# Seven-product groups of a hybrid layer: sums made in three PSUM banks, product order turned

## The chip, the cores and the metric

The kernel runs on one core of one Trainium2 chip. The metric is device time in microseconds (us) of one execution. The engines are called as the profile calls them: PE is the matrix engine, DVE the vector engine, ACT the scalar engine, POOL and SP the two others (here mostly queues that issue transfers). PSUM is the memory into which PE writes its products, in banks of 128 partitions x 512 fp32 numbers.

## The reference, cut to what matters

One layer on 512 tokens of 2048 channels, fp32 in and out. The projection `h @ w_in` has 7 x 1024 columns; half of the layer is a causal depthwise convolution of width 31, the other half attention with 16 heads of 64.

```python
h = rms_norm(x, norm_g)
z = h @ w_in                       # (512, 2048) @ (2048, 7168)
a_val, a_glu, a_gate, q, k, v, b_gate = jnp.split(z, SPLIT_POINTS, axis=-1)
u = causal_depthwise_conv(a_val * sigmoid(a_glu), conv_w, conv_b)
u = silu(layer_norm(u)) @ conv_pw_w + conv_pw_b
y_a = u * silu(a_gate)
q, k = rms_norm per head of q and k
o = dilated_attention_mixture(q, k, v)   # three dilated windows, mixed
y_b = o * silu(b_gate)
y = x + concat(y_a, y_b) @ w_out
```

## The kernel before

**Tiles and groups.** Everything stays on the core: tokens lie in 16 tiles of 128 channels x 512 tokens (`x16`). The columns of `w_in`, of the pointwise matrix and of `w_out` are worked off in groups of 512 columns, named by `GROUPS`: four of the gated value (`vg`, 0 to 3), then `q0`, `k0`, `v0`, a gate, the second halves, the pointwise groups and the output. A group of `w_in` has four units of 512 x 512 weights (1 MB each), which SP fetches into a ring of eight tiles `wf`. Products are made in fp16 with each operand as a high and a low part: `tri` issues three matmuls (high x high, high x low, low x high), L411, L412 and L413. For the high parts ACT copies with a scale (`hi`, L1128), for the low parts DVE subtracts (`lo`; every DVE instruction passes through a helper and has L80).

**Seven products.** Three groups, `vg3`, `q0` and `v0`, cut x and the weights into 2 x 2 blocks and make seven block products in place of eight (Strassen's scheme in Winograd's form), in `input_products`. s1 to s4 are sums of weight blocks, t1 to t4 sums of blocks of x (made early by `sum_x`, on DVE). Each product has two pairs of units and, in each, two halves m of 128 columns or tokens: 4 pieces of 12 matmuls of 256 columns. One piece is one *slot*. So such a group has 28 slots, and slot 4n + 2 pair + m holds piece (pair, m) of product n. Each product has a bank of its own out of the four of `lin_ps`. Results leave the bank by an ACT copy (L1180) or a DVE operation that also adds, and the four output blocks are then put together by DVE.

**What sets the order.** The order is written by hand. The list `plan` in `input_products` gives each step a slot relative to the group's first; `after(n, fn)` enters it into a calendar that is worked off clock by clock, and all engines execute in the order in which the calendar issued their instructions. In one clock the steps of the calendar are issued ahead of the matmuls that come later in `plan`. `hi` of a weight block stands five slots ahead of its product, `lo` four (the second product's first half one later). Three of the four weight sums are made by POOL as adding transfers (`nc.gpsimd.dma_start` with `accum_op`, L1122), s1 by DVE.

**The filler.** The convolution is 30 steps for each of 8 tiles on DVE (`cv<-u,cw,cv`, one multiply-add each), issued by `run_conv` wherever the class `Weighed` thinks that DVE has room: each DVE instruction adds 180 plus its size to a load, each clock takes 1230 (later 1480) off it, and conv steps are issued while it is below zero. The sum of the convolution's tiles (`lnacc`) ends in one matmul for the mean, L568.

**q and k.** `norm_qk` makes the per-head norm: a square (ACT, L1242 in `q0`, L510 in `k0`), a sum (DVE, `ss`), mean and epsilon on POOL (L478), a power on POOL (L168), a scaling (DVE), the high part (ACT, `qhl`, L486), the low part (DVE), then transposing transfers issued by SP, one for each part.

Of the kernel before, what the change touches and what calls it, by code (L numbers as in the profile page):

```python
# [70 lines left out]
class Weighed:  # L71
# [5 lines left out]
    def __getattr__(self, name):  # L77
        def call(out, src, *args, **kw):
            self.load += START + max(math.prod(a.shape[1:]) for a in (out, src) if hasattr(a, "shape"))
            return getattr(self.engine, name)(out, src, *args, **kw)  # L80
        return call
# [3 lines left out]
def layer(ctx: ExitStack, tc: tile.TileContext, xt, w1, w2, w3, g_in, conv_w, conv_b,  # L85
# [273 lines left out]
    xn, tx = {}, {}  # L359

    def sum_x(j):
# [9 lines left out]
        V.tensor_sub(t4, b21, t2)
        both = lambda t: t.rearrange("p (n t) -> p n t", n=2)

        def high():
            for n, t in ((0, t12), (2, t34)):
                A.activation(to[:, n:n + 2, 0], both(t), AF.Copy)

        def low():
# [30 lines left out]
    def tri(ps, a, b, first, last):  # L409
        (ah, al), (bh, bl) = a, b  # L410
        T.matmul(ps, ah, bh, start=first, stop=False)  # L411
        T.matmul(ps, ah, bl, start=False, stop=False)  # L412
        T.matmul(ps, al, bh, start=False, stop=last)  # L413
# [53 lines left out]

    by_head = lambda t: t.rearrange("p (h d) -> p h d", d=DH)

    def norm_qk(store, z, sq, n, to):  # L470
# [13 lines left out]
        def high():  # L484
            got["hl"] = temp("qhl", F16, [P, 2, S])
            A.activation(got["hl"][:, 0], z, AF.Copy)  # L486

        def low():
            hl_t = got["hl"]
            V.tensor_tensor(hl_t[:, 1], z, hl_t[:, 0], op=OP.subtract)  # L490
            for part in range(2):
                if store not in qk:
                    qk[store] = [wide_tile("qk4", [P, 4, S], F16) for _ in range(2)]
                to(qk[store][part], hl_t[:, part])
# [610 lines left out]

    def input_products(i0):
# [9 lines left out]
        def add(name, pair):
            if name == "s1":
                V.tensor_tensor(block("a11", pair), block("a22", pair), block("a11", pair), op=OP.subtract)
            else:
                x, to = SUMS[name]  # L1120
                if name in BY_DMA:
                    nc.gpsimd.dma_start(block(to, pair), block(x, pair), accum_op=OP.add)  # L1122
                else:
# [26 lines left out]
        order = [("p1", "a11", "b11"), ("u", "a22", "t4"), ("x", "a12", "b21"), ("p7", "s3", "t3"), ("p5", "s1", "t1"),  # L1150
                 ("p6", "s2", "t2"), ("z", "s4", "b22")]
        u_first = group != SEVEN[0]
        if u_first:
            order[:2] = order[1::-1]

        def product(n, pair, m):
            to, w, x = order[n]
            if (pair, m) == (0, 0):
                bank[to] = lin_ps.tile([P, 2, H], F32, name="ps_l", tag="ps_l")
            ps, ms = bank[to][:, m], slice(m * P, (m + 1) * P)  # L1160
            for k in range(KU):
                t, xs = weights[w, pair], x_part(x, pair, k)
                first, last_ = pair == m == k == 0, pair == m == 1 and k == KU - 1
                if by_token:
                    tri(ps, [x[:, ms] for x in xs], (t[:, 0, k], t[:, 1, k]), first, last_)
                else:
                    tri(ps, [t[:, j, k, ms] for j in range(2)], xs, first, last_)
# [10 lines left out]
        def copy(name):  # L1178
            t = got[name] = slot("cb")
            A.activation(t, bank.pop(name).rearrange("p m t -> p (m t)"), AF.Copy, scale=e["p"])  # L1180

        def stt(out, name, by, other, op):
            V.scalar_tensor_tensor(out, bank[name].rearrange("p m t -> p (m t)"), e[by], other, op0=OP.mult, op1=op)

        def first_block():
            got["11"] = slot("cb")
            stt(got["11"], "x", "p", got["p1"], OP.add)
            bank.pop("x")

        def joint():  # L1190
            q, h = got["p1"], got["p7"]
            stt(q, "p6", "p", q, OP.subtract)
            bank.pop("p6")
# [261 lines left out]
```

## Time and profile before

| what | before |
| --- | --- |
| median of 3 runs | 817.36 us (817.11 to 817.39) |
| profiled execution, first to last instruction (span) | 815.8 us |
| PE busy | 807.9 us, 99% |
| DVE busy | 707.1 us, 87% |
| ACT busy | 553.6 us, 68% |
| POOL busy | 138.1 us, 17% |
| granted PE clock | 0.999 |

Of the profiled execution the span is what is recorded; the 1.56 us between it and the median lie ahead of the first and behind the last instruction. A line of a timeline reads: start, duration, engine, line, operation, output<-inputs, sizes, and in brackets how long the engine was idle before it and on whom it waited. Successive instructions of one engine overlap a little at their ends, so the distance between two starts is what counts.

### The profile page before, as it was taken

The numbers are of one execution on the slowest core, as the hardware profiler recorded it, in microseconds if no ns is written. First come the engines' busy times: TensorE is split into PE (matmuls) and PEld (weight loads), VectorE is DVE, ScalarE is ACT, GpSimd is POOL, SyncE is SP. The second block draws the span as 40 slices with busy tenths as digits, with TensorE's granted clock in tenths as the row PEclk, the third lists the DMA queues.
The fourth block names the chain that finished last, engine by engine and source line by source line (L and its number), as shares of the span: only waits on it lengthen the run. The fifth ranks groups of instructions, "written<-read, shape, count | busy, mean of one in ns | idle before, by whom it ended". The sixth has DMA issues, their size and how long they took to land.

```text
span 815.8 us, 13495 instructions
## 1 busy us (share of the span) xinstructions
PE 807.9 (99%) x5271; PEld 500.6 (61%) x5271; DVE 707.1 (87%) x1181; ACT 553.6 (68%) x778; POOL 138.1 (17%) x159
## 2 busy tenths in 40 slices
PE   9999999999999999999999999999999999999998
PEld 6887645888646864444444444444444444788887
DVE  6768999889888989999999988996677798998985
ACT  6667687567656678677756748487688858766540
POOL 0001020413223500004112010010110002412420
PEclk9999999999999999999999999999999999999999
DMA  9953343995675862537473632536343477578752
GB/s 341 344 215 102 105 110 98 132 279 113 261 143 114 156 252 98 122 104 174 136 181 100 172 105 86 134 104 168 104 117 104 136 236 234 116 176 189 130 104 66
DMA packets 98625, 125.62 MB, mean 154 GB/s; under 512 B 62720, under 2 KB 83968, under 8 KB 89344
## 3 DMA queue, kind: packets, MB, share of 16 engines
q1 hardware_dynamic: 80800, 107.38, 41.9%
q0 software_dynamic: 17472, 17.30, 14.9%
q8 instruction: 41, 0.67, 0.3%
q14 instruction: 24, 0.20, 0.1%
q10 hardware_dynamic: 288, 0.07, 0.0%
HBM read 88.56 MB, written 4.19 MB: 114 GB/s over the span
## 4 chain that ended last, share of the span: by engine, by line
PE 69%; DVE 19%; ACT 5%; issue 3%; DMA 3%; POOL 1%; SPq 0%; ACTq 0%; DVEq 0%; POOLq 0%
PE ps_l L411 17%; PE ps_l L412 17%; PE ps_l L413 16%; PE ps_l L879 10%; DVE cv L80 6%; DVE wl L80 3%; DVE ws L80 3%; ACT junk L190 2%; PE ps_s L413 2%; PE ps_s L411 2%; PE ps_s L412 2%; PE ps_s L723 2%; PE ps_o L763 2%; DMA wf<-w_dram 1%; DVE cb L80 1%
## 5 line engine op out<-in xcount | busy, mean ns | idle before, releaser
L80 DVE SCALAR_TENSOR_TENSOR cv<-u,cw,cv 128x511 f32<-128x511 f32 (+14 forms) x240 | 162.2, 728 | 0.4 <-ACT cv L544 0.4
L190 ACT ACTIVATE junk<-wf 128x2048 uint8<-128x2048 f32 x68 | 129.2, 1900 | 3.5 <-DMA wf<-w_dram 3.1
L411 PE MATMUL ps_l<-x,wh 128*128 128x512 f16 x320 | 121.4, 379 | 0.3 <-DVE glu L80 0.3
L413 PE MATMUL ps_l<-x,wl 128*128 128x512 f16 x320 | 121.3, 379 | 0.0
L412 PE MATMUL ps_l<-x,wh 128*128 128x512 f16 x320 | 121.3, 379 | 0.0
L299 ACT ACTIVATE wh<-wf,ws 128x2048 f16<-128x2048 f32 x44 | 87.7, 1993 | 49.0 <-PE ps_l L412 49.0
L80 DVE SCALAR_TENSOR_TENSOR wl<-wf,ws,wh 128x2048 f16<-128x2048 f32 x45 | 105.6, 2347 | 13.0 <-ACT wh L299 13.0
L411 PE MATMUL ps_l<-wh,x 128*128 128x512 f16 x256 | 97.1, 379 | 0.0
L412 PE MATMUL ps_l<-wl,x 128*128 128x512 f16 x256 | 97.1, 379 | 0.0
L413 PE MATMUL ps_l<-wh,x 128*128 128x512 f16 x256 | 97.0, 379 | 0.0
L80 DVE SCALAR_TENSOR_TENSOR ws<-wf,ws 128x1024 f16<-128x1024 f32 x70 | 89.0, 1278 | 7.5 <-ACT ws L1128 4.9
L411 PEld LDWEIGHTS <-wh 128*128 128x128 f16 x480 | 47.0, 98 | 55.4 <-issue 3.5
L413 PEld LDWEIGHTS <-wl 128*128 128x128 f16 x480 | 46.9, 98 | 53.6 <-DVE wl L80 0.4
L412 PEld LDWEIGHTS <-wh 128*128 128x128 f16 x480 | 46.9, 98 | 50.4 <-issue 0.7
L879 PE MATMUL ps_l<-xr,wr 128*128 128x512 f32 x288 | 69.7, 397 | 0.1
L204 POOL TENSOR_SCALAR ws<-ws 128x1 f32<-128x1 f32 x22 | 10.7, 485 | 341.8 <-DVE ws L80 313.0
L879 PEld LDWEIGHTS ps_l<-xr,wr 128*128 128x128 f32 x288 | 54.1, 189 | 13.8 <-ACT xr L338 1.0
L413 PEld LDWEIGHTS <-x 128*128 128x128 f16 x352 | 34.4, 98 | 32.8 <-issue 1.5
L411 PEld LDWEIGHTS <-x 128*128 128x128 f16 x352 | 34.4, 98 | 32.4 <-issue 1.9
L412 PEld LDWEIGHTS <-x 128*128 128x128 f16 x352 | 34.4, 98 | 30.6 <-issue 0.5
L946 ACT ACTIVATE ws<-wf,ws 128x1024 f16<-128x1024 f32 x28 | 32.1, 1147 | 28.7 <-PE ps_l L413 9.4
L1128 ACT ACTIVATE ws<-wf,ws 128x1024 f16<-128x1024 f32 x42 | 46.4, 1138 | 6.1 <-PE ps_l L413 3.9
(250 smaller groups left out, 1823.3 us busy)
## 6 DMA issues: line engine op xcount, KB each, us to landing
wf<-w_dram SPq DMA_DIRECT2D x72, 1024.0 KB, 5.2
wf<-wf POOLq DMA_DIRECT2D x30, 512.0 KB, 6.5
x<-xt_dram SPq DMA_DIRECT2D x16, 256.0 KB, 6.7
res<-xt_dram SPq DMA_DIRECT2D x8, 512.0 KB, 6.5
out_dram<-res SPq DMA_DIRECT2D x15, 256.0 KB, 2.2
wf<-w_dram SPq DMA_DIRECT2D x7, 512.0 KB, 7.2
wf<-wf POOLq DMA_DIRECT2D x6, 256.0 KB, 6.3
qk<-qhl SPq DMA_TRANSPOSE x40, 3.0
```

The costliest lines, as they stand in the source:

```text
L80: return getattr(self.engine, name)(out, src, *args, **kw)
L190: A.activation(junk[:, :n], src, AF.Square, scale=scale, accum_out=acc)
L204: G.tensor_scalar(scale, scale, 1e-30, 2.0 ** (-2 * top), op0=OP.max, op1=OP.mult)
L299: A.activation(parts[i][0], raw[i], AF.Copy, scale=wscale[units[i][3:]][0])
L411: T.matmul(ps, ah, bh, start=first, stop=False)
L412: T.matmul(ps, ah, bl, start=False, stop=False)
L413: T.matmul(ps, al, bh, start=False, stop=last)
L723: T.matmul(ps[i, a], qk["q", hf][q][rows, p4, i * P:w], qk["k", hf][k][rows, p4, :w], start=n == 0, stop=n == 2)
L763: T.matmul(po[rows, i * P:(i + 1) * P], vs[hf][j // 2][:, j % 2, 2 * p4 + a, vp * DH:(vp + 1) * DH], got["t", a][:, pp * (ALL // P) + FROM ...
L879: T.matmul(banks[group, m], wt[:, a, m * P:(m + 1) * P], xk[b], start=k == 0 and a == b == 0, stop=k == KC - 1 and a == 1)
L946: A.activation(t[:, 0], block(name), AF.Copy, scale=wscale["wa", g][0])
L1128: A.activation(t[:, 0], block(name, pair), AF.Copy, scale=wscale[group][0])
```

## The change

In the three groups the seven products are made in the order a11 b11, a12 b21, s1 t1, s2 t2, s3 t3, s4 b22, a22 t4, in three banks A, C, B, A, A, B, A. A bank is no longer emptied after each product: products 4, 5 and 7 are added by PE to what stands in A, product 6 to what stands in B. What is needed of the partial sums is copied out between: A after product 1 (`p1`), B after product 3 (`p5`), A after product 4 (`u2`, in two copies of 256 columns at slots 15 and 16, while slots 15 and 16 are the last piece of product 4 and the first of product 5), A after product 5 (`nw`), A at the end. DVE combines three times per group instead of seven. The signs of t2, t3, t4 change with it, so `sum_x` has two multiply-subtract operations where it had an add and a subtract; t1 and t2 now lie in tiles of one pool, t3 and t4 in tiles of another. The weight sums are s1, s2 and s4 by transfers and s3 by DVE; s2 is now at slots 0 and 1. `hi` and `lo` of the second product's first half come one slot earlier. The measuring of newly fetched weights is spread (offsets 0, -1, +2, +3).

For q and k the high and the low part lie side by side in one tile, and one transpose takes both; mean and epsilon go from POOL to DVE. `Weighed` counts 90 for operations under 256 numbers and 25/24 of the size.

```diff
-            self.load += START + max(...)
+            n = max(math.prod(a.shape[1:]) for a in (out, src) if hasattr(a, "shape"))
+            self.load += (START if n >= H else START // 2) + n * 25 // 24
...
-        V.tensor_sub(t3, b12, b22)
-        V.tensor_add(t2, b22, t1)
-        V.tensor_sub(t4, b21, t2)
+        V.tensor_sub(t3, b22, b12)
+        V.scalar_tensor_tensor(t2, t1, -1.0, b22, op0=OP.mult, op1=OP.subtract)
+        V.scalar_tensor_tensor(t4, t2, -1.0, b21, op0=OP.mult, op1=OP.subtract)
...
+    def turn_qk(to, t, src):
+        nc.sync.dma_start(to[:, :, :, t * P:(t + 1) * P].rearrange("p d h t -> p (d h) t"),
+                          src.rearrange("p d h t -> p (d h t)"), transpose=True)
...
-            G.tensor_scalar(ss, ss, f / DH, f * RMS_EPS, op0=OP.mult, op1=OP.add)
+            V.tensor_scalar(ss, ss, f / DH, f * RMS_EPS, op0=OP.mult, op1=OP.add)
...
+    IN_SUMS = {"s1": ("a22", "a21"), "s2": ("a21", "a11"), "s4": ("a11", "a12")}
+    IN_PLACE = {"s1": "a21", "s2": "a11", "s3": "a21", "s4": "a12"}
+    ORDER = (("A", "a11", "b11"), ("C", "a12", "b21"), ("B", "s1", "t1"), ("A", "s2", "t2"), ("A", "s3", "t3"),
+             ("B", "s4", "b22"), ("A", "a22", "t4"))
...
-            if (pair, m) == (0, 0):
+            if to not in bank:
                 bank[to] = lin_ps.tile([P, 2, H], F32, name="ps_l", tag="ps_l")
...
-                    after(MEASURE, lambda j=j: measure(i0 + j + RING))
+                    after(MEASURE + (0, -1, 2, 3)[j], lambda j=j: measure(i0 + j + RING))
...
+        def copy(to, name, by="p", f=0, n=S):
+            if f == 0:
+                got[to] = slot("cb")
+            A.activation(got[to][:, f:f + n], flat(name)[:, f:f + n], AF.Copy, scale=e[by])
+
+        def joint(to, name, other):
+            got[to] = got.pop(other)
+            V.scalar_tensor_tensor(got[to], flat(name), e["p"], got[to], op0=OP.mult, op1=OP.add)
+            bank.pop(name)
+
+        def fourth():
+            p5 = got.pop("p5")
+            got["22"] = got.pop("nw")
+            V.tensor_tensor(got["22"], got["22"], p5, op=OP.subtract)
+
+        def third():
+            copy("21", "A", "n")
+            bank.pop("A")
...
-                norm_qk(group, t, sq, [(2, 4, 5, 6), (2, 5, 6, 8), (3, 8, 9, 11), (2, 9, 10, 12)][n], to)
+                norm_qk(group, t, sq, (2, 5, 6, 8), to)
...
+        plan = [(2, scales_of), (4, lambda: copy("p1", "A")), (8, lambda: joint("11", "C", "p1")), (18 if kind == "v" else 9, lambda: out("11")),
+                (12, lambda: copy("p5", "B")), (15, lambda: copy("u2", "A", n=H)), (16, lambda: copy("u2", "A", f=H, n=H)),
+                (20, lambda: copy("nw", "A", "n")), (21, fourth), (22, lambda: out("22")),
+                (24, lambda: joint("12", "B", "u2")), (25, lambda: out("12")), (28, third), (29, lambda: out("21"))]
...
-                at = 4 * n + 2 * pair - 5 + ((n, pair) == (1, 0))
+                at = 4 * n + 2 * pair - 5
```

How the instructions stand now is shown at three places. On PE in `vg3`, around slot 16 of the group (`tx` are the sums of x, `ws` the weight parts, L411 to L413 before and L413 to L415 now the three matmuls of `tri`; the last rows of one slot and the first of the next). Before:

```order
L411 MATMUL ps_l<-tx,ws 128x256
L412 LDWEIGHTS ws
L412 MATMUL ps_l<-tx,ws 128x256
L413 LDWEIGHTS ws
L413 MATMUL ps_l<-tx,ws 128x256
L411 LDWEIGHTS ws [waits Activation_49]
L411 MATMUL ps_l<-tx,ws 128x256 [waits PE_49]
L412 LDWEIGHTS ws
L412 MATMUL ps_l<-tx,ws 128x256
L413 LDWEIGHTS ws [waits DVE_49]
```

And now:

```order
L413 MATMUL ps_l<-tx,ws 128x256
L414 LDWEIGHTS ws
L414 MATMUL ps_l<-tx,ws 128x256
L415 LDWEIGHTS ws
L415 MATMUL ps_l<-tx,ws 128x256
L413 LDWEIGHTS ws
L413 MATMUL ps_l<-tx,ws 128x256 [waits Activation_49]
L414 LDWEIGHTS ws
L414 MATMUL ps_l<-tx,ws 128x256
L415 LDWEIGHTS ws [waits DVE_49]
```

Before, the slot's first weight load waited for the weight part that ACT makes five slots ahead, and the matmul only for PE's own earlier work. Now the matmul itself waits for ACT, and what it waits for is the copy of the `u2` half that is issued just ahead of it. The same row with the same wait stands 12 matmuls earlier, at the start of slot 15, and both stand again in `q0` and in `v0`: six rows in all.

On ACT in `q0`, around its slots 12 to 17 (L1180 and L1189 empty a bank, L1128 and L1138 are `hi`, L486 and L494 the high part of q; L190 and L191 measure fetched weights). Before:

```order
L1242 ACTIVATE sq<-cb 128x512 [waits DVE_49]
L1128 ACTIVATE ws<-wf,ws 128x1024 [waits PE_49,Activation_49]
L1128 ACTIVATE ws<-wf,ws 128x1024 [waits DMASW0_49,PE_49,Activation_49]
L1180 ACTIVATE cb<-ps_l,esc 128x512 [waits PE_49]
L486 ACTIVATE qhl<-cb 128x512 [waits DVE_49]
L1128 ACTIVATE ws<-wf,ws 128x1024 [waits DMASW1_49,Activation_49]
```

And now:

```order
L1189 ACTIVATE cb<-ps_l,esc 128x512 [waits PE_49]
L1138 ACTIVATE ws<-wf,ws 128x1024 [waits DVE_49,Activation_49]
L494 ACTIVATE qhl<-cb 128x4x128 [waits DVE_49]
L1189 ACTIVATE cb<-ps_l,esc 128x256 [waits PE_49]
L1138 ACTIVATE ws<-wf,ws 128x1024 [waits DMASW2_49,Activation_49]
L1189 ACTIVATE cb<-ps_l,esc 128x256 [waits PE_49]
```

The first of the two `u2` copies stands right behind `qhl`, which waits for DVE; before, `qhl` stood behind the copy.

On DVE at the start of `v0` (`z` and `ss` belong to `k0`, whose last results are then taken out of PSUM; `ws<-wf,ws` are `lo` of the first products of `v0`). Before:

```order
L80 SCALAR_TENSOR_TENSOR z<-ps_l,esc,qg 128x512 [waits PE_49]
L80 SCALAR_TENSOR_TENSOR ws<-wf,ws 128x1024 [waits DMAHW5_49,Activation_49]
L80 SCALAR_TENSOR_TENSOR cv<-u,cw,cv 128x484 [waits DVE_49]
L80 SCALAR_TENSOR_TENSOR z<-ps_l,esc,qg 128x512 [waits PE_49]
L80 SCALAR_TENSOR_TENSOR cv<-u,cw,cv 128x483 [waits DVE_49]
L80 SCALAR_TENSOR_TENSOR ws<-wf,ws 128x1024 [waits DMAHW6_49,Activation_49]
L80 SCALAR_TENSOR_TENSOR ws<-wf,ws 128x1024 [waits DMAHW4_49,Activation_49]
```

And now:

```order
L81 SCALAR_TENSOR_TENSOR z<-ps_l,esc,qg 128x512 [waits PE_49]
L81 SCALAR_TENSOR_TENSOR ws<-wf,ws 128x1024 [waits DMAHW2_49,Activation_49]
L81 SCALAR_TENSOR_TENSOR z<-ps_l,esc,qg 128x512 [waits PE_49]
L81 SCALAR_TENSOR_TENSOR ws<-wf,ws 128x1024 [waits DMAHW1_49,Activation_49]
L81 SCALAR_TENSOR_TENSOR cv<-u,cw,cv 128x482
L81 SCALAR_TENSOR_TENSOR ws<-wf,ws 128x1024 [waits DMAHW3_49,Activation_49]
```

The third `ws` (the first half of the second product) stands a slot earlier, and one conv step in place of two lies between the rows shown.

More of the change, by code (lines that the diff above doesn't have):

```diff
@@ L32 @@
 LP = 4
+H = S // 2
 WARM = 9
@@ L406, in token_rsqrt, with tri @@
         A.activation(row, ps, AF.Copy)
-    def tri(ps, a, b, first, last):
+    def tri(ps, a, b, first, last, more=False):
         (ah, al), (bh, bl) = a, b
-        T.matmul(ps, ah, bh, start=first, stop=False)
-        T.matmul(ps, ah, bl, start=False, stop=False)
-        T.matmul(ps, al, bh, start=False, stop=last)
+        T.matmul(ps, ah, bh, start=first, stop=False, skip_group_check=more)
+        T.matmul(ps, ah, bl, start=False, stop=False, skip_group_check=more)
+        T.matmul(ps, al, bh, start=False, stop=last, skip_group_check=more)
     u, cv, bg, ag = {}, {}, {}, {}
@@ L484, in high @@
         def high():
-            got["hl"] = temp("qhl", F16, [P, 2, S])
-            A.activation(got["hl"][:, 0], z, AF.Copy)
+            got["hl"] = temp("qhl", F16, [P, NT, 2, P])
+            A.activation(got["hl"][:, :, 0], by_block(z), AF.Copy)
         def low():
             hl_t = got["hl"]
[L490 to L494, printed above, removed]
+            V.tensor_tensor(hl_t[:, :, 1], by_block(z), hl_t[:, :, 0], op=OP.subtract)
+            if store not in qk:
+                qk[store] = [wide_tile("qk4", [P, 2, 2, S], F16) for _ in range(2)]
+            to(qk[store], hl_t)
         for m, fn in zip(n, (reduce, scale, high, low)):
@@ L514, in evac_qk @@
         norm_qk(("k" if is_k else "q", half_i), z, sq, n,
-                lambda to, src: nc.sync.dma_start(to[:, :, t * P:(t + 1) * P], src, transpose=True))
+                lambda to, src: [turn_qk(to[x], t, src[:, 2 * x:2 * x + 2]) for x in range(2)])
     vscale = {}
@@ L722, in scores @@
                     for a, rows in enumerate(halves):
-                        T.matmul(ps[i, a], qk["q", hf][q][rows, p4, i * P:w], qk["k", hf][k][rows, p4, :w], start=n == 0, stop=n == 2)
+                        T.matmul(ps[i, a], qk["q", hf][p4 // 2][rows, p4 % 2, q, i * P:w],
+                                 qk["k", hf][p4 // 2][rows, p4 % 2, k, :w], start=n == 0, stop=n == 2)
             for i in order:
@@ L1148, in x_part @@
             return [t[:, f:f + H] for t in x16[8 * pair + 4 * (name[1] == "2") + k]]
[L1150 to L1154, printed above, removed]
         def product(n, pair, m):
[L1157 to L1158 removed]
+            to, w, x = ORDER[n]
+            if to not in bank:
                 bank[to] = lin_ps.tile([P, 2, H], F32, name="ps_l", tag="ps_l")
             ps, ms = bank[to][:, m], slice(m * P, (m + 1) * P)
+            opens = n == [o[0] for o in ORDER].index(to)
             for k in range(KU):
                 t, xs = weights[w, pair], x_part(x, pair, k)
[L1163 removed]
+                first, last_ = opens and pair == m == k == 0, pair == m == 1 and k == KU - 1
                 if by_token:
[L1165 removed]
+                    tri(ps, [x[:, ms] for x in xs], (t[:, 0, k], t[:, 1, k]), first, last_, not opens)
                 else:
[L1167 removed]
+                    tri(ps, [t[:, j, k, ms] for j in range(2)], xs, first, last_, not opens)
         def scales_of():
@@ L1176, in scales_of @@
             e.update(p=p, n=n)
[L1178 to L1193, printed above, removed]
-            V.tensor_tensor(h, h, q, op=OP.add)
-        def fifth():
-            got["22"] = slot("cb")
-            stt(got["22"], "p5", "n", got["p7"], OP.add)
-            stt(got["p1"], "p5", "p", got["p1"], OP.subtract)
-            bank.pop("p5")
-            got["12"] = got.pop("p1")
-        def sixth():
-            t = got["21"] = got.pop("u")
-            V.tensor_tensor(t, t, got.pop("p7"), op=OP.add)
-        def final():
-            stt(got["12"], "z", "p", got["12"], OP.add)
-            bank.pop("z")
+        flat = lambda name: bank[name].rearrange("p m t -> p (m t)")
+        def copy(to, name, by="p", f=0, n=S):
[13 more added lines that the diff above has]
+            bank.pop("A")
         count = [0]
```

51 lines of the change are left out of this document (22 added, 29 removed).

## The prediction, made before the run

> **What bounds the kernel now.** I read the page's first part, then PE's waits, then the three changed groups as windows. The page:
>
> ```profile
> span 815.8 us, 13495 instructions
> PE 807.9 (99%) x5271; PEld 500.6 (61%) x5271; DVE 707.1 (87%) x1181; ACT 553.6 (68%) x778; POOL 138.1 (17%) x159
> ```
>
> PE is busy 99% of the span, and the change leaves it the same matmuls. So an edit gains only where PE now stands still, and loses wherever it makes PE stand still. The list of PE's waits (who waited <- for whom: us, times, longest) says where it does:
>
> ```profile
> PE ps_l L412 <- DVE ws L80: 1.8, 2, 1.1
> PE ps_s L568 <- DVE lnacc L80: 0.8, 1, 0.8
> PE ps_l L411 <- ACT ws L1128: 0.4, 1, 0.4
> PE ps_l L411 <- DVE glu L80: 0.3, 1, 0.3
> ```
>
> These 3.3 us are all that stands in the list after PE's start. Short waits hide behind matmuls whose modelled ends overlap, so I also compare the three groups, which have the same 336 matmuls (window, its length, busy time of PE, PEld, DVE, ACT, POOL, granted clock, DMA share, GB/s):
>
> ```profile
> 138.60:175.30 36.70, 36.70 (x338) 32.86 (x337) 33.48 (x42) 20.89 (x22) 10.86 (x9) 1.00 0.85 189
> 175.30:212.00 36.70, 36.70 (x339) 32.85 (x337) 32.13 (x40) 24.95 (x28) 9.69 (x9) 1.00 0.68 151
> 253.50:293.20 39.70, 37.45 (x338) 32.79 (x337) 34.19 (x42) 25.16 (x30) 18.35 (x15) 1.00 0.82 188
> ```
>
> `vg3` and `q0` run without a gap: 36.70 us are 28 slots of 1.31, a matmul each 0.109. `v0` takes 3.00 us more. With the mean's wait (0.8) and the glu wait (0.3) the most that any edit can give back is 4.1 us.
>
> **The change, part by part.**
>
> *Six new waits.* At slots 15 and 16 of each group PE's first matmul waits for the copy of half of bank A, and the copy waits for the slot before to end. Nothing can overlap: PE stops, ACT copies, PE goes on. What that costs is put together from these rows, the end of a slot in `vg3` and the copy behind it, and the ACT groups by form (count | busy, mean ns | idle):
>
> ```profile
> 149.00 0.27 PE L413 MATMUL ps_l<-tx,ws 128*128 128x256 f16 x1
> 149.11 0.27 PE L411 MATMUL ps_l<-x,ws 128*128 128x256 f16 x1
> 149.31 0.69 ACT L1180 ACTIVATE cb<-ps_l,esc 128x512 f32<-128x512 f32 x1 [1.47 <-PE ps_l L413]
> ```
>
> ```profile
> L746 ACT ACTIVATE hl<-sx,st 128x512 f16<-128x512 f32 x16 | 11.3, 708 | 0.0
> L746 ACT ACTIVATE hl<-sx,st 128x256 f16<-128x256 f32 x16 | 7.9, 493 | 0.0
> L1180 ACT ACTIVATE cb<-ps_l,esc 128x512 f32<-128x512 f32 x6 | 4.1, 677 | 4.2 <-PE ps_l L413 4.2
> L1180 ACT ACTIVATE cb<-ps_l 128x512 f32<-128x512 f32 x3 | 1.8, 586 | 0.4 <-PE ps_l L413 0.4
> ```
>
> From the start of the slot's last matmul (149.00) to the copy's start are 0.31. A copy of 512 columns takes 0.677 with a scale from memory (`vg3`, `q0`) and 0.586 with a constant one (`v0`); 256 columns fewer are worth 0.708 - 0.493 = 0.215, so half a copy is 0.46 or 0.37. PE's restart is seen at `v0`'s present stall:
>
> ```profile
> 255.06 1.28 DVE L80 SCALAR_TENSOR_TENSOR ws<-wf,ws 128x1024 f16<-128x1024 f32 x1 [1.24 <-ACT ws L1128]
> 256.10 0.27 PE L411 MATMUL ps_l<-ws,tx 128*128 128x256 f16 x1
> 256.40 0.27 PE L412 MATMUL ps_l<-ws,tx 128*128 128x256 f16 x1
> ```
>
> DVE ends at 256.34, PE starts at 256.40: 0.05. Less the pitch that would have passed anyway (0.11), a stall is 0.31 + 0.46 + 0.05 - 0.11 = 0.71, in `v0` 0.62. Four and two of them: **+4.1**. Bounds: 0.5 each if the copy's end is overlapped (3.0), 0.93 each if a half costs as much as a whole (5.3).
>
> The wait's row in the order names the bank's reader, though half 0 is read while half 1 is written. The Trainium skill, "PSUM — Partial Sum Buffer", section "PSUM bank collisions raise a hardware error", says why: PE and another engine must not touch one bank in the same quarter of the partitions at once, different columns included, so waits go by bank and not by address. No row here shows PE writing into a bank that ACT reads at that moment; by address the result would be the first rival's, by bank it is mine.
>
> *Late copies.* The 0.71 holds only if ACT is free when the slot ends. In `q0` the first copy now stands behind `qhl`, whose chain begins at slot 8 with DVE's addition to bank C. PE and its followers in `q0` today (the last matmul of slot 14, then the steps that the chain is made of), and for DVE's operations two rows from elsewhere:
>
> ```profile
> 194.88 0.27 PE L413 MATMUL ps_l<-ws,tx 128*128 128x256 f16 x1
> 195.00 0.68 DVE L80 TENSOR_REDUCE ss<-sq 128x8 f32<-128x512 f32 x1
> 197.06 2.02 POOL L168 TENSOR_TENSOR ss<-ss,half 128x8 f32<-128x8 f32 x1
> 199.11 0.69 DVE L80 TENSOR_TENSOR cb<-cb,ss 128x512 f32<-128x512 f32 x1 [1.54 <-POOL ss L168]
> 199.83 0.63 ACT L486 ACTIVATE qhl<-cb 128x512 f16<-128x512 f32 x1 [2.62 <-DVE cb L80]
> ```
>
> ```profile
> 266.41 1.21 DVE L80 TENSOR_TENSOR wf<-wf 128x1024 f32<-128x1024 f32 x1
> L80 DVE SCALAR_TENSOR_TENSOR cb<-ps_l,esc,cb 128x512 f32<-128x512 f32 x8 | 5.9, 743 | 0.0
> ```
>
> Bank C is complete seven slots before 194.88, at 185.7, and DVE can start at 186.0. The order then gives DVE, ahead of the scaling, the addition (0.74), two s3 sums (1.21 each), two `lo` (1.28 each), the sum of squares (0.68) and the small mean operation (0.15): 192.6. POOL's power 2.02, the scaling 0.69, `qhl` 0.63: 195.9. The copy could have begun at 194.88 + 0.31 = 195.2. So it is 0.7 late at best; a conv step that is still ahead of it on DVE costs 0.65 more, and the hand-overs 0.1. I take **+1.1** (0 to 2.5). In `v0` each of the two copies has one `qhl` ahead of it that waits for DVE: half a `qhl` for the first and a whole one for the second, 0.3 + 0.6 = **+0.9** (0 to 2). In `vg3` nothing stands ahead of the copies but a `hi` that is issued earlier: 0.
>
> *The stalls in `v0` go.* They come from a DVE that arrives late. It takes the second tile of `k0` out of PSUM at 250.64, though PE was done at 248.4:
>
> ```profile
> 248.09 0.38 PE L413 MATMUL ps_l<-wh,x 128*128 128x512 f16 x1
> 250.64 0.74 DVE L80 SCALAR_TENSOR_TENSOR z<-ps_l,esc,qg 128x512 f32<-128x512 f32 x1
> 259.45 0.27 PE L411 MATMUL ps_l<-ws,x 128*128 128x256 f16 x1 [0.35 <-ACT ws L1128]
> 260.77 0.27 PE L412 MATMUL ps_l<-ws,x 128*128 128x256 f16 x1 [1.05 <-DVE ws L80]
> 272.39 0.27 PE L412 MATMUL ps_l<-ws,tx 128*128 128x256 f16 x1 [0.74 <-DVE ws L80]
> ```
>
> Behind it wait, on ACT, the square, a measuring and `hi`, and then `lo`: the stalls at 256.40, 259.45 and 260.77. With the change PE is there 4 x 0.71 + 1.1 = 3.9 us later. DVE's list from the start of `vg3` to that `z` is 1.6 us shorter (counted in the order, with the rows' durations: 7 combinations of 0.7 per group become 3, and conv steps fill most of the room), and its waits for ACT in `k0` shift by less than PE does. So the lag of 2.2 us is used up. The third `lo` is also a slot (1.31) earlier, and the last stall, at 272.39, is the same lag not yet made up. I take all of it: **-3.0** (0 to -3.0).
>
> *The mean's matmul.* PE waits for the last sum of the convolution:
>
> ```profile
> 546.04 1.42 DVE L80 TENSOR_TENSOR lnacc<-lnacc,cv 128x512 f32<-128x512 f32 x2
> 546.34 0.38 PE L413 MATMUL ps_l<-x,wl 128*128 128x512 f16 x1
> 547.50 0.70 PE L568 MATMUL ps_s<-lnacc,ones 128*128 128x512 f32 x1 [0.79 <-DVE lnacc L80]
> 516.91 7.82 DVE L80 SCALAR_TENSOR_TENSOR cv<-u,cw,cv 128x497 f32<-128x497 f32 x12
> ```
>
> It costs 547.50 - 546.34 - 0.21 = 0.95. DVE now has 5 conv steps fewer ahead of that sum since its last wait (492): 5 x 0.65 = 3.2 us; the matmul is issued two slots earlier, 2.6 us. 0.6 of the wait goes: **-0.65** (0 to -0.95).
>
> *What costs nothing.* Four of `sum_x`'s operations more expensive by some 0.04 each (multiply-subtract 743 against 687 for 512 columns) stand ahead of the glu wait, which has no slack: **+0.15**. The other combinations that DVE is spared (4 per group) are hidden now, since PE doesn't wait there; conv steps take their place. POOL's 16 mean operations and SP's 8 transposes are waited for by nobody on PE's path before; uncovered, a transpose would cost its landing, 3 us. ACT's extra copies fit into its 32% of idle time, except where they are counted above.
>
> **Sum:** 4.1 + 1.1 + 0.9 - 3.0 - 0.65 + 0.15 = +2.6. On the profiled span that is 815.8 -> 818.4; the runs' median stands 1.56 above the span, so the time is 817.36 + 2.6 = **819.9**.
>
> **Rivals.**
>
> 1. *The copies run beside PE.* If the halves really overlap (the reader of half 0 is done before PE needs the bank), neither stalls nor lateness exist: -3.0 - 0.65 + 0.15 = -3.5, **813.9**, faster. For it: half a copy, 0.46, is far shorter than a slot, 1.31, and reads columns that the running slot doesn't write. Against it: the rows of the order, in which PE's matmul waits for that copy. It decides if the start of slot 15 comes 0.11 after the end of slot 14 in all three groups. Chance 0.04.
> 2. *Six bare stalls.* Not slower within what can be told: ACT reaches the copies in time, because DVE is ahead in `q0` and the chain through POOL ends before 195.2. Then 4.1 - 3.0 - 0.65 + 0.15 = +0.6, **818.0**. For it: without four combinations per group, DVE is lighter. Against: the chain's own steps are 0.7 too long without any conv step. It decides if the first copy of `q0` starts within 0.4 of its slot's last matmul. Chance 0.27.
> 3. *The lag stays.* DVE fills what it is spared with conv steps and comes to `v0` as late as before: of the 3.0 only half goes, and `q0`'s copy is 2.5 late: 4.1 + 2.5 + 0.9 - 1.5 - 0.65 + 0.15 = +5.5, **822.9**. For it: `run_conv` fills any room that the load model sees. Against: PE comes 3.9 later. Chance 0.12.
> 4. *The mechanism as forecast*, 818.7 to 821.2. Chance 0.57.
>
> **How the numbers follow.** What a measurement can tell from no change is 0.2%, 1.6 us: slower begins at 819.0, faster ends at 815.7. Case 4 is slower but for a seventh of it (0.49 and 0.08), case 2 is the same but for 0.05, case 3 slower, case 1 faster. Slower 0.66, same 0.30, faster 0.04. The range from 817.6 to 822.4 takes in case 4, two thirds of case 2 and a little of case 3.
>
> **What would show it.** In PE's waits six rows behind ACT's `cb` copies, each 0.5 to 1.7 long, and none in the three groups before slot 15. `vg3` takes 38.1 us, `q0` 39.2, `v0` 38.8. ACT starts the first copy of `q0` some 1 us after PE stops, right behind `qhl`. DVE's `z` in `k0` starts 0.3 after its matmuls. The mean's wait is 0.3 or less. I am wrong if `vg3` takes 36.7 (no stalls), or if `v0` still has waits for `ws`.

## The result, and the profile after

The changed kernel took 821.88 us (median of 4 runs, 820.65 to 822.08), the kernel before 817.38 (4 runs): a ratio of 1.005, 95% interval 1.0036 to 1.0064. It is slower by 4.5 us; forecast were 2.6, a time of 819.9 and a range of 817.6 to 822.4. The profiled execution has a span of 820.3 us, 4.5 above the 815.8 of before, so it shows the whole difference. Its page, and the list of PE's waits beside PE's start:

```profile
span 820.3 us, 13455 instructions
PE 809.1 (99%) x5271; PEld 501.3 (61%) x5271; DVE 702.3 (86%) x1185; ACT 557.9 (68%) x787; POOL 131.8 (16%) x143
PE ps_l L413 <- ACT cb L1189: 5.8, 6, 2.2
PE ps_l L887 <- ACT xr L338: 0.5, 1, 0.5
PE ps_l L413 <- DVE glu L81: 0.3, 1, 0.3
```

DVE has 4.8 us less to do, and yet the kernel is slower. The waits for `ws` and for `lnacc` are gone from the list. In their place stand six waits for the copies of a bank (`cb`), 5.8 us that the list sees. The three groups, in windows of their own (length, busy PE, PEld, DVE, ACT, POOL, granted clock, DMA share, GB/s):

```profile
138.90:177.10 38.20, 37.08 (x339) 32.94 (x338) 33.24 (x42) 22.24 (x25) 11.55 (x11) 1.00 0.91 195
177.10:218.10 41.00, 38.20 (x338) 33.36 (x337) 33.37 (x43) 27.81 (x32) 10.06 (x10) 0.96 0.69 161
259.60:298.40 38.80, 36.97 (x338) 32.84 (x337) 34.60 (x45) 25.02 (x30) 14.21 (x11) 1.00 0.88 195
```

`vg3` takes 38.2 us (it was 36.7), `q0` 41.0 (36.7), `v0` 38.8 (39.7). In `q0` the granted clock is 0.96, which no group showed before. First the end of slot 14 in `vg3`, from ACT's and PE's timelines:

```profile
158.44 0.27 PE L415 MATMUL ps_l<-tx,ws 128*128 128x256 f16 x1
158.75 0.47 ACT L1189 ACTIVATE cb<-ps_l,esc 128x256 f32<-128x256 f32 x1 [2.21 <-PE ps_l L415]
159.28 0.27 PE L413 MATMUL ps_l<-tx,ws 128*128 128x256 f16 x1 [0.56 <-ACT cb L1189]
```

PE's last matmul starts at 158.44, the copy 0.31 later, takes 0.47, and PE starts again at 159.28: 0.84 in place of 0.11, a stall of 0.73. The same place in `q0`:

```profile
187.07 1.38 DVE L81 SCALAR_TENSOR_TENSOR cv<-u,cw,cv 128x501 f32<-128x501 f32 x2
188.37 0.74 DVE L81 SCALAR_TENSOR_TENSOR cb<-ps_l,esc,cb 128x512 f32<-128x512 f32 x1
194.66 2.64 POOL L169 TENSOR_TENSOR ss<-ss,half 128x8 f32<-128x8 f32 x1 [8.93 <-DVE ss L81]
198.06 0.63 ACT L494 ACTIVATE qhl<-cb 128x512 f16<-128x512 f32 x1 [3.39 <-DVE cb L81]
196.59 0.27 PE L415 MATMUL ps_l<-ws,tx 128*128 128x256 f16 x1
198.60 0.46 ACT L1189 ACTIVATE cb<-ps_l,esc 128x256 f32<-128x256 f32 x1
199.10 0.37 PE L413 MATMUL ps_l<-ws,tx 128*128 128x256 f16 x1 [2.24 <-ACT cb L1189]
199.27 0.42 PE L414 MATMUL ps_l<-ws,tx 128*128 128x256 f16 x1
```

The copy could have begun at 196.9 and begins at 198.60, right behind `qhl`: 1.7 late, and PE's stall is 199.10 - 196.59 - 0.11 = 2.4. Then the matmuls come every 0.21 instead of 0.11 (0.42 in place of 0.27 for one), 11 of them in about 2.3 us: the clock is halved, which costs another 1.1. The second stall of `q0` is 0.87, those of `v0` 0.88 and 1.28.

### The profile page after: what moved, and what is told of

Read it like the earlier page. It is cut to its first block, busy times and chain, and to the rows that moved or that the text cites. A ratio compares the mean times of both kernels' runs of the same rounds, so it can differ in the third digit from the quotient of the medians.

```text
span 820.3 us, 13455 instructions
## 1 busy us (share of the span) xinstructions
PE 809.1 (99%) x5271; PEld 501.3 (61%) x5271; DVE 702.3 (86%) x1185; ACT 557.9 (68%) x787; POOL 131.8 (16%) x143
## 4 chain that ended last, share of the span: by engine, by line
PE 84%; DVE 12%; issue 2%; ACT 1%; DMA 1%; POOL 0%; SPq 0%; DVEq 0%; ACTq 0%
PE ps_l L413 22%; PE ps_l L415 22%; PE ps_l L414 22%; PE ps_l L887 10%; DVE cv L81 4%; PE ps_s L415 2%; PE ps_s L413 2%; PE ps_s L414 2%; DVE ws L81 2%; DVE wl L81 2%; PE ps_s L730 2%; PE ps_o L771 2%; DMA x<-xt_dram 1%; DVE sx L81 1%; DVE z L81 0%
## 5 line engine op out<-in xcount | busy, mean ns | idle before, releaser
L191 ACT ACTIVATE junk<-wf 128x2048 uint8<-128x2048 f32 x68 | 129.2, 1900 | 1.6 <-DMA wf<-w_dram 1.2
L413 PE MATMUL ps_l<-x,wh 128*128 128x512 f16 x320 | 121.3, 379 | 0.3 <-DVE glu L81 0.3
L415 PE MATMUL ps_l<-x,wl 128*128 128x512 f16 x320 | 121.3, 379 | 0.0
L413 PE MATMUL ps_l<-wh,x 128*128 128x512 f16 x256 | 97.1, 379 | 0.0
L415 PE MATMUL ps_l<-wh,x 128*128 128x512 f16 x256 | 97.0, 379 | 0.0
L413 PEld LDWEIGHTS <-wh 128*128 128x128 f16 x480 | 47.0, 98 | 55.3 <-issue 4.0
L415 PEld LDWEIGHTS <-wl 128*128 128x128 f16 x480 | 46.9, 98 | 53.6 <-DVE wl L81 0.4
L413 PEld LDWEIGHTS <-x 128*128 128x128 f16 x352 | 34.4, 98 | 32.5 <-issue 1.9
L415 PEld LDWEIGHTS <-x 128*128 128x128 f16 x352 | 34.4, 98 | 31.3
L1138 ACT ACTIVATE ws<-wf,ws 128x1024 f16<-128x1024 f32 x42 | 47.6, 1140 | 8.4 <-PE ps_l L415 6.8
L169 POOL TENSOR_TENSOR ss<-ss,half 128x8 f32<-128x8 f32 x16 | 32.2, 2012 | 122.2 <-DVE ss L81 122.0
```

Source lines behind the costliest of these rows:

```text
L169: G.tensor_tensor(ap, ap, half.to_broadcast(list(ap.shape)), op=OP.pow)
L191: A.activation(junk[:, :n], src, AF.Square, scale=scale, accum_out=acc)
L413: T.matmul(ps, ah, bh, start=first, stop=False, skip_group_check=more)
L415: T.matmul(ps, al, bh, start=False, stop=last, skip_group_check=more)
L1138: A.activation(t[:, 0], block(name, pair), AF.Copy, scale=wscale[group][0])
```

## The experiments

Stalls are given as the distance between two starts of matmuls, less the usual pitch.

**Product a12 b21 moved between s2 t2 and s3 t3.** If a bank rests for a product before PE writes it again, the copies should cost nothing. The edit, with the weight sums where the new order needs them:

```diff
-ORDER = (("A", "a11", "b11"), ("C", "a12", "b21"), ("B", "s1", "t1"), ("A", "s2", "t2"), ("A", "s3", "t3"),
+ORDER = (("A", "a11", "b11"), ("B", "s1", "t1"), ("A", "s2", "t2"), ("C", "a12", "b21"), ("A", "s3", "t3"),
          ("B", "s4", "b22"), ("A", "a22", "t4"))
-    ..., (8, lambda: joint("11", "C", "p1")), (18 if kind == "v" else 9, lambda: out("11")),
-    (12, lambda: copy("p5", "B")), (15, lambda: copy("u2", "A", n=H)), (16, lambda: copy("u2", "A", f=H, n=H)), ...
+    ..., (16, lambda: joint("11", "C", "p1")), (18 if kind == "v" else 17, lambda: out("11")),
+    (8, lambda: copy("p5", "B")), (12, lambda: copy("u2", "A")), ...
-    ... (-6, "s1", 0), (-5, "s1", 1), (0, "s2", 0), (1, "s2", 1), (8, "s3", 0), (10, "s3", 1), (6, "s4", 0), (7, "s4", 1)
+    ... (-8, "s1", 0), (-7, "s1", 1), (-3, "s2", 0), (-1, "s2", 1), (8, "s3", 0), (10, "s3", 1), (9, "s4", 0), (11, "s4", 1)
```

> The changed kernel with product a12 b21 (bank C) moved from the second to the fourth place: A, B, A, C, A, B, A. Every bank that is read in between now rests for a whole product (4 slots) before PE writes it again; one whole copy of u2. All else as in the change, the weight sums some slots earlier. In the changed kernel's trace the six stalls cost 1.46 (vg3), 3.28 (q0) and 2.16 us (v0), and a drop of PE's clock behind q0's long stall another 1.07: 8.0 us in all. Theory 1 (the stalls are the reads of a bank that PE writes on at once, and v0's old stalls went only because PE came later): no wait of PE for a copy, clock 1.00 in q0, vg3 and q0 36.7 us each, but old waits of PE for ws come back in v0, 1 to 3 us: 815 to 817. Theory 2 (v0's old stalls went by the new order itself): v0 36.7 too, 813.9. Theory 3 (the stalls come from the ACT queue as a whole): PE still waits for copies, 819 or more.

Measured: 817.95 us (ratio to before 1.000, 0.999 to 1.0009), span 815.5. PE waits for no copy. The windows of `vg3`, `q0`, `k0` and `v0`, and then PE's wait at the start of `k0` with what it waits for:

```profile
138.80:175.50 36.70, 36.70 (x338) 32.87 (x337) 33.01 (x42) 22.35 (x24) 10.81 (x10) 1.00 0.84 189
175.50:212.20 36.70, 36.65 (x336) 32.54 (x335) 28.77 (x37) 26.60 (x29) 9.52 (x8) 1.00 0.71 161
212.20:256.60 44.40, 41.68 (x198) 19.07 (x196) 39.38 (x57) 26.21 (x28) 12.12 (x10) 1.00 0.65 161
256.60:293.30 36.70, 36.70 (x337) 32.69 (x336) 32.26 (x41) 25.04 (x30) 15.67 (x11) 1.00 0.79 169
213.33 2.34 DVE L81 SCALAR_TENSOR_TENSOR wl<-wf,ws,wh 128x2048 f16<-128x2048 f32 x1
215.72 0.38 PE L414 MATMUL ps_l<-wl,x 128*128 128x512 f16 x1 [2.72 <-DVE wl L81]
```

The windows are set by hand; from matmul start to matmul start `vg3` and `v0` take 36.7 us and `q0` 37.1, with two waits of 0.19 that are too short for the list.

What theories 1 and 2 have in common holds: the stalls were the reads of a bank that PE writes on at once, and they go to zero. (Copying `u2` in one piece, which this kernel does too, isn't enough for that, as a run below shows.) `v0` runs in 36.7, so its old stalls didn't come back. But a new one of 2.9 us stands where none was forecast: `q0`'s norm steps now fall together at its end, and DVE comes to the first weights of `k0` late. So this run alone can't tell whether `v0` is clean by itself or because PE lost 2.9 us just ahead.

**The same, with q0's norm steps spread.** The first block's scaling, high and low part go 2, 4 and 4 slots later, two outputs 3 and 1 slots, and two conv steps are held back:

```diff
-norm_qk(group, t, sq, (2, 5, 6, 8), to)
+norm_qk(group, t, sq, (2, 7, 10, 12) if n == 0 else (2, 5, 6, 8), to)
-(22, lambda: out("22")), ..., (25, lambda: out("12"))
+(25 if kind == "q" else 22, lambda: out("22")), ..., (26 if kind == "q" else 25, lambda: out("12"))
+if kind == "q":
+    plan += [(n, lambda d=d: setattr(V, "load", V.load + d)) for n, d in ((20, 1400), (26, -1400))]
```

> The kernel with bank C between s2 t2 and s3 t3 (no copy waits; span 815.5 us) lost 2.9 us at the first weights of k0: DVE began their low part at 213.3, behind q0's norm steps and two conv steps, with PE there at 212.6. Here q0's norm steps are moved: the first block's scaling, high and low part 2, 4 and 4 slots later, the second and third block's output 3 and 1 slots later, and two conv steps held back for six slots. Theory (that wait is DVE's and ACT's burst at the end of q0 alone): the low part starts by 211.6, no wait at k0, span 815.5 - 2.9 = 812.6, 814.4. If v0's start is then late, since PE gets there 2.9 earlier, up to 2.5 come back: 816.9. Rival (the lag is DVE's total load, and only moves on): 817 to 818.

Measured: 815.35 us (6 runs, 813.89 to 815.8), ratio to before 0.9969 (0.9957 to 0.998): faster than both kernels. The windows of `vg3`, `q0`, `v0` and all that PE waits for beside its start:

```profile
139.20:175.90 36.70, 36.70 (x338) 32.89 (x337) 33.03 (x42) 22.35 (x24) 10.80 (x10) 1.00 0.84 189
175.90:212.60 36.70, 36.56 (x337) 32.60 (x335) 30.08 (x37) 26.92 (x30) 9.51 (x8) 1.00 0.73 174
254.10:291.60 37.50, 37.18 (x339) 32.86 (x337) 32.23 (x41) 25.23 (x31) 15.47 (x12) 1.00 0.78 157
PE ps_l L414 <- DVE ws L81: 0.3, 1, 0.3
PE ps_l L413 <- DVE glu L81: 0.3, 1, 0.3
```

The wait at `k0` is gone. The span is 814.0 in the profiled run, 1.4 more than expected: from matmul start to matmul start `q0` takes 37.0 and `v0` 37.35, not 36.7, with small waits for `ws`, and PE's start differs by 0.4. Here PE is late by no more than the 0.3 of `q0` when it comes to `k0`, and still 2.4 of the 3.1 us of old stalls are gone. DVE takes the second tile of `k0` out of PSUM here:

```profile
249.79 0.75 DVE L81 SCALAR_TENSOR_TENSOR z<-ps_l,esc,qg 128x512 f32<-128x512 f32 x1
```

That is 36.9 us after `k0`'s first matmul (212.93); before the change it was 38.6 (250.64 and 212.02).

**u2 copied in one piece.**

```diff
-..., (15, lambda: copy("u2", "A", n=H)), (16, lambda: copy("u2", "A", f=H, n=H)), ...
+..., (16, lambda: copy("u2", "A")), ...
```

> The changed kernel with u2 copied in one piece of 512 columns at slot 16 instead of two halves at 15 and 16: three waits instead of six. Theory (a half costs nearly the whole, since start 0.31, restart 0.05 and the wait by bank stay): vg3 0.93, q0 0.93 and some 0.4 of lateness behind qhl and no drop of the clock, v0 0.84 and 0.3; together 3.4 instead of 8.0 us. If v0's old stalls went only because PE is late, 1 to 2 us of them come back: 818.5 to 819.5; if not, 817.3. Rival (the halves do overlap with PE in part, and the first wait is q0's and v0's ACT queue alone): vg3 stays at 38.2 us and the time at 821 or above.

Measured: 822.88 us, 1 us above the change. The three stalls are 0.94 in `vg3`, as worked out, but 2.35 in `q0` and 2.38 in `v0`. The reason for the long ones is in ACT's timeline of `q0`:

```profile
197.20 0.63 ACT L494 ACTIVATE qhl<-cb 128x512 f16<-128x512 f32 x1 [3.39 <-DVE cb L81]
197.74 1.13 ACT L1138 ACTIVATE ws<-wf,ws 128x1024 f16<-128x1024 f32 x1
198.78 0.67 ACT L1189 ACTIVATE cb<-ps_l,esc 128x512 f32<-128x512 f32 x1
```

The copy is a slot later in the queue, and so a weight part of 1.13 is ahead of it too. My expectation had left that instruction out. Where ACT was free, three whole copies would be cheaper than six halves (3 x 0.94 against 6 x 0.73); where it wasn't, the place in the queue decided. Even so the three stalls are 5.7 us together, against 6.9 for the six of the change. The time is longer by the clock behind them, which is 0.996 in three of the four runs (822.85 to 823.27), and the profiled execution, the fourth, has 0.998 and 821.08. That the time lies where the rival put it is not the rival's mechanism, since the stalls of `vg3` went from 1.46 to 0.94.

**q0's first high part behind the first copy.**

```diff
-norm_qk(group, t, sq, (2, 5, 6, 8), to)
+norm_qk(group, t, sq, (2, 5, 8, 10) if n == 0 else (2, 5, 6, 8), to)
```

> The changed kernel with the high part of the first q block two slots later on ACT (8 instead of 6 after its square), so behind both u2 copies in q0. Theory (q0's first copy is late because it stands behind qhl, and the clock drops because that stall is 2.4 us long): q0's two stalls are 0.72 each and the granted clock in q0 is 1.00, so q0 takes 38.2 instead of 41.0 us, 819.0; where PE's earlier arrival brings v0's old stalls back, up to 2 more, 821. Rival (the copy is late for another reason, or the clock drops by itself): q0 stays at 40 to 41 us, 821.9.

Measured: 819.13 us (10 runs), as expected. (The low part moves by the same two slots.) `q0`, the second window, and ACT there, where `qhl` now lies between the two copies and delays neither:

```profile
176.80:215.00 38.20, 37.07 (x340) 32.92 (x339) 33.22 (x43) 27.81 (x32) 10.18 (x10) 1.00 0.68 162
196.72 0.47 ACT L1189 ACTIVATE cb<-ps_l,esc 128x256 f32<-128x256 f32 x1 [2.23 <-PE ps_l L415]
198.13 0.62 ACT L494 ACTIVATE qhl<-cb 128x512 f16<-128x512 f32 x1
198.75 0.47 ACT L1189 ACTIVATE cb<-ps_l,esc 128x256 f32<-128x256 f32 x1
```

Both stalls are 0.73, and the clock is 1.000 in each of the ten runs. `v0` still has only its copies' stalls, though PE reaches it 2.9 us earlier than in the change, counted from the start of `vg3`. DVE's first two extractions of `k0`, in the change:

```profile
252.07 0.75 DVE L81 SCALAR_TENSOR_TENSOR z<-ps_l,esc,qg 128x512 f32<-128x512 f32 x1 [1.02 <-PE ps_l L415]
254.59 0.75 DVE L81 SCALAR_TENSOR_TENSOR z<-ps_l,esc,qg 128x512 f32<-128x512 f32 x1 [0.51 <-PE ps_l L415]
```

And in this run:

```profile
248.96 0.75 DVE L81 SCALAR_TENSOR_TENSOR z<-ps_l,esc,qg 128x512 f32<-128x512 f32 x1 [1.02 <-PE ps_l L415]
251.48 0.75 DVE L81 SCALAR_TENSOR_TENSOR z<-ps_l,esc,qg 128x512 f32<-128x512 f32 x1 [0.51 <-PE ps_l L415]
```

DVE waits for PE just as long in both. It isn't PE's coming later that gives DVE this slack: DVE and ACT in `q0` shift with PE.

**The same in v0.** The high and low parts of `k0`'s last two blocks go 5 and 3 slots later, too.

```diff
-n = [..., 11 + 2 * t + 2 * (t > 0), 13 + 2 * t + 2 * (t > 0)]
+n = [..., 11 + 2 * t + 2 * (t > 0) + (0, 0, 5, 3)[t], 13 + 2 * t + 2 * (t > 0) + (0, 0, 5, 3)[t]]
```

> The run before last's idea carried to v0: the changed kernel with q0's first high part behind the u2 copies, and now also the high parts of k0's last two blocks 5 and 3 slots later, behind v0's two copies. Theory (v0's two stalls of 0.88 and 1.28 are the bare 0.62 each plus the lateness behind those high parts): 0.62 twice in v0, 0.92 less than 819.1: 818.2. Rival (they are late behind the weight parts): v0 keeps 2.16, 819.1.

Measured: 818.15 us (10 runs). The two stalls of `v0` are 0.64 each, and the list shows six bare ones:

```profile
PE ps_l L413 <- ACT cb L1189: 3.2, 6, 0.6
```

From 821.88 to 819.13 to 818.15: the lateness behind high parts, with the clock, costs the change 3.7 us. What is left of the six stalls is 4 x 0.73 + 2 x 0.64 = 4.2.

**A long stall put into vg3.** Three more copies ahead of the first half copy, on top of the kernel with q0's high part later.

```diff
-..., (15, lambda: copy("u2", "A", n=H)), ...
+..., (15, lambda: ([copy("u2", "A") for _ in range(3)] if kind == "vg" else None, copy("u2", "A", n=H))), ...
```

> The changed kernel with q0's first high part behind the u2 copies (819.1, the granted clock 1.000 in all ten of its runs), and in vg3 three more whole copies of u2 ahead of the first half copy, which are thrown away: the stall of PE there grows from 0.73 by 3 x 0.58 to 2.45. Theory (a stall of over 2 us makes PE's clock drop for some 2 us behind it, wherever it is, in some of the runs, by where a measuring window falls): 820.9 where it doesn't, 822 to 823 where it does, granted clock 0.996 to 0.998 in a third or more of the runs. Rival (the drop belongs to q0's state, POOL and DVE busy): clock 1.000 in all runs and 820.9.

Measured: 822.05 us; granted clock 0.998 in three of four runs (821.9 to 822.4), 1.000 in the fourth (821.05). In the profiled run PE stands 2.46, runs one slot at full speed (its last matmul starts 1.19 after its first), and is then at half speed:

```profile
160.66 0.27 PE L413 MATMUL ps_l<-tx,ws 128*128 128x256 f16 x1 [2.29 <-ACT cb L1189]
161.85 0.37 PE L415 MATMUL ps_l<-tx,ws 128*128 128x256 f16 x1
162.79 0.37 PE L413 MATMUL ps_l<-tx,ws 128*128 128x256 f16 x1 [0.56 <-ACT cb L1189]
162.96 0.42 PE L414 MATMUL ps_l<-tx,ws 128*128 128x256 f16 x1
```

So the drop follows a long stall also in `vg3`, where there are no steps of q. In the windows of `vg3` shown above, with stalls of 0.73 or none, the clock was 1.00.

**The old load model in the change.**

```diff
-self.load += (START if n >= H else START // 2) + n * 25 // 24
+self.load += START + max(math.prod(a.shape[1:]) for a in (out, src) if hasattr(a, "shape"))
```

> The changed kernel with the old load model of the filler (180 plus the size for every operation). Theory (v0's old stalls went because the products leave DVE less to do, not because of the load model): v0 has no wait for ws, 39.1 us, and the whole is 821.9 within 1. Rival (the new load model holds conv steps back ahead of v0): waits for ws in v0 again, 823 to 825.

Measured: 822.77 us. `v0` has no wait for `ws`, so the load model isn't what removed them. The mean's wait is 0.80 instead of 0.28, and the first of `v0`'s copy stalls 1.44 instead of 0.88.

**The second product's first half one slot later, as before.**

```diff
-at = 4 * n + 2 * pair - 5
+at = 4 * n + 2 * pair - 5 + ((n, pair) == (1, 0))
```

> The changed kernel with the high and low part of the second product's first half one slot later, as it was. In the changed kernel's v0 that low part ends at 262.2, and PE needs it at 264.6. Theory (a slot of 1.3 is covered by this margin of 2.4): no new wait, 821.9. Rival (v0's stall of 1.2 at that product went by this edit): a wait for ws at the second product in v0, 1 us, 823.

Measured: 823.41 us in one run, 1.3 more span than the change. It isn't the wait that the rival named: at the second product PE doesn't wait. But further on `v0` has a wait of 0.39 for a later `ws`, and its first copy stall is 1.69 instead of 0.88, 1.2 together. In this run the slot was worth more than its margin said; that all that follows on ACT and DVE moves with it is my reading, and there is no second run of this kernel.

**The q and k part alone, in the kernel before.** Products and load model are as before.

```diff
-G.tensor_scalar(ss, ss, f / DH, f * RMS_EPS, op0=OP.mult, op1=OP.add)
+V.tensor_scalar(ss, ss, f / DH, f * RMS_EPS, op0=OP.mult, op1=OP.add)
...
-got["hl"] = temp("qhl", F16, [P, 2, S])
+got["hl"] = temp("qhl", F16, [P, NT, 2, P])
...
-nc.sync.dma_start(store[:, 2 * x:2 * x + 2, f:f + P], src[:, m * H:(m + 1) * H], transpose=True)
+turn_qk(store[x], 2 * z + m, src[:, 2 * m:2 * m + 2])
```

> The kernel before with only the q and k part of the change: one transpose for both parts, mean and epsilon on DVE. Theory (hidden, nobody on PE's path waits for them; DVE has some 16 x 0.1 us more and the load model issues a few conv steps later): 817.4, within 0.5. Rival (16 DVE operations of the old load model push conv steps and so change v0's stalls or the mean's wait): 816 or 819.

Measured: 819.49 us, ratio 1.0022 (1.0012 to 1.0031): slower, where I had expected nothing, and about what the rival said. New in its list of PE's waits:

```profile
PE ps_s L573 <- DVE lnacc L80: 1.0, 1, 1.0
PE ps_l L412 <- DVE u L80: 0.8, 2, 0.4
PE ps_l L411 <- ACT u L314: 0.5, 1, 0.5
```

`v0` keeps two waits for `ws`, 2.3 us. The mean's matmul comes at 553.7 instead of 547.5, and pointwise matmuls wait for the normed convolution. The filler has got behind.

**All but the products.** The run before, with the new load model added.

```diff
-self.load += START + max(math.prod(a.shape[1:]) for a in (out, src) if hasattr(a, "shape"))
+n = max(math.prod(a.shape[1:]) for a in (out, src) if hasattr(a, "shape"))
+self.load += (START if n >= S // 2 else START // 2) + n * 25 // 24
```

> The kernel before with the q and k part and the new load model, but its own seven products. The q and k part alone measured 819.5: 1.8 us of it were new waits of the pointwise matmuls for the normed convolution, because sixteen small DVE operations count 188 each in the old model and push the conv steps back. Theory (the new model counts them less and takes the conv steps up again): those waits go, v0's 2 to 3 us stay, 817.5 within 0.8. Rival (the DVE time itself does it): 819 or above.

Measured: 832.37 us, 15 above before. My theory of a remedy was wrong: the new model slows the filler further, not the other way. Up to DVE's second extraction of `k0`, counted from `vg3`, 46 conv steps are issued, where there were 49 in the run before.

```profile
PE ps_s L406 <- DVE diag L81: 4.3, 1, 4.3
PE ps_s L574 <- DVE lnacc L81: 2.7, 1, 2.7
PE ps_l L412 <- ACT u L315: 1.9, 3, 1.2
PE ps_l L413 <- DVE ws L81: 1.3, 2, 1.0
```

The mean's matmul is another 7 us later (560.4), and the layer norm behind it keeps PE waiting 4.4 us, with half the clock after each long wait. That the 25/24 on every large operation is what does it is argued from the code, not shown alone. What is shown: the new load model goes with the lighter products, not with the old ones; and `v0`'s waits for `ws` stay in both kernels that have the old products.

## Why the prediction was right, and where it was not

By the terms of the sum (the measured ones from the two profiled executions, from the distances between matmuls):

| term | forecast | measured |
| --- | --- | --- |
| six bare stalls | +4.1 | +4.2 |
| q0's copies late | +1.1 | +1.8 |
| v0's copies late | +0.9 | +0.9 |
| clock halved behind q0's stall | none | +1.1 |
| v0's old stalls | -3.0 | -3.1 |
| the mean's matmul | -0.65 | -0.67 |
| glu wait | +0.15 | 0.0 |
| PE's start (waits for `xr`) | none | +0.3 |
| sum | +2.6 | +4.5 |

The time lies in the range, but above the 818.7 to 821.2 that the forecast mechanism was to give; the one run of the change without a drop of the clock, 820.65, lies inside. The sums have two small slips: 817.36 + 2.6 is 820.0, not 819.9, and the upper bound of the six stalls comes to 5.4, not 5.3. `vg3` starts between 138.5 and 139.2 in the twelve profiles, so the 0.3 at PE's start need not belong to the change. The glu wait is 0.3 in both lists: what was added to it in the forecast didn't come.

*Six new waits.* Right in mechanism and size: 0.73 against 0.71, 0.64 against 0.62, with half copies of 0.47 and 0.36. The order with bank C in between shows that it is the read of a bank on which PE goes on at once: zero there. That the wait goes by bank and not by columns is what the order and the six stalls show; a kernel without that wait wasn't tried.

*Late copies.* Right in mechanism: `qhl` ahead of the copy, as the two runs with it later show. In `q0` the size was off: 1.8 for 1.1. The chain had the steps that were forecast. DVE's addition to bank C began at 188.37, 0.7 after it could have (slot 7's last matmul starts at 187.40, and 0.31 more make 187.7), behind a conv step, of which the forecast had put in about half; and POOL's power took 2.64 instead of 2.02 (its 16 executions take 1.6 to 2.6 in both kernels, so one row was a poor price).

*The clock.* The step that failed by leaving out: I priced a stall at its own length. Behind 2.4 us PE ran 11 matmuls at half speed, 1.1 more. That, with the 0.7 of `q0`, is most of the missing 1.9. The Trainium skill, "TensorE: Matmul & The Clock Gate", Part 1, states that the clock is halved after an idle window of about 3.4 us, and that the windows run freely, not from the kernel's start. The second fits the runs (three of four drop, the fourth doesn't); the length doesn't: here 2.2 to 2.3 us of waiting were enough, and by 3.4 the change would have had no drop at all.

*The stalls in v0.* The right size, and of the two reasons given one is enough. I said that PE comes 3.9 us later and that DVE's list up to its `z` in `k0` is 1.6 us shorter. The second holds as it was counted: from the start of `vg3` to that `z` DVE is busy 98.1 us instead of 99.7, with 54 conv steps instead of 50. The first wasn't needed. With PE 2.9 earlier than in the change the stalls stayed away, and DVE's slack was the same. With PE late by 0.3 alone 2.4 of 3.1 were still gone. How late DVE takes up that tile and what `v0` loses go together: 38.6 us after `k0`'s first matmul in the kernel before (3.1 lost), 37.9 and 37.3 in the two other kernels with the old products (2.3 and 1.7), 36.9 with the norm steps spread (0.65), and 36.5 in the change, where it waits for PE (nothing). So the most of it is the new products, by what they spare DVE; ACT is not spared (25.4 us busy in `k0`, 24.5 before). The old load model brought no wait back. The earlier slot of the second product's weight parts has a share, 1.2 in one run; what the moved weight sums and the spread measuring have in it wasn't tried alone.

*The mean's matmul.* As forecast, to 0.02.

*What costs nothing.* The q and k part was put at nothing. Alone it costs 1.8 us, by the filler that it delays. In the change none of these waits is left; that the lighter products give the filler more room than the q and k part takes is the likely reason, and not shown alone.

*The rivals.* The first (copies beside PE, 813.9) falls with the six rows. The second (bare stalls, 818.0) is what the kernel with both high parts later measures, 818.15: it was a kernel of its own, not this one. The third (the lag stays, 822.9) came near in time, by another way: its `v0` stalls didn't stay.

## What to carry to other kernels

A bank that PE goes on accumulating in can be read in between without a wait of PE, if another product is put between the read and the next write; moving one product so took away all six stalls. Where PE does wait for an engine's copy, look at what stands ahead of the copy in that engine's queue, and follow its chain back: the queue cost here as much as the copies. And a part that is hidden can still cost by the filler that it pushes back, so try such parts alone before they are called free.

## What the runs showed that I had not expected

PE's clock was halved for some 2 to 3.5 us after stalls of 2.4 us and more, in some runs and not in others. With stalls up to 1.28 all 10 runs of one kernel, and 10 of another with 0.73 at most, had a clock of 0.999 or 1.000. With 2.4 us (`q0` of the change, `vg3` with added copies) it was 0.998 in three of four runs each, and these are 0.8 to 1.4 us longer than the fourth run of the same kernel. In the kernel with two such stalls three of four runs had 0.996. The drop can begin at once (199.10 in the change) or a slot later (161.85 with the added copies). It can also stay away: the stall of 2.4 in `q0` left none in the profiled execution with the old load model (clock 1.000), nor did that of 2.9 in the run with bank C in between, though five of its ten runs had 0.997 or 0.998. In the profiled executions the drop cost 1.1 us on a stall of 2.4 (`q0` of the change) and 1.7 on another of 2.4 (`v0` with one copy), so a long stall is dearer than its length. Between 1.28 and 2.35 the runs have stalls of 1.44 and 1.69 alone, in two kernels that also have one of 2.4, so where the drop begins stays open.
